# LayerNorm with GELU on one core: batch 3 loaded in one DMA, and 64 bytes written into the result by each DMA engine at the start

## The chip, the core and the metric

The kernel runs on one core of one Trainium2 chip. The metric is the device time of one execution in microseconds (us), less is better. Each number of a kernel is a median over several executions; repeated runs of one kernel here lie within 0.3% of each other, but for one run of 321.24 us.

## The reference

```python
# x: 8 x 1024 x 2048 float32; gamma, beta: 2048
mean = np.mean(x, axis=-1, keepdims=True)
var = np.var(x, axis=-1, keepdims=True)
normalized = (x - mean) / np.sqrt(var + eps)
out = gamma * normalized + beta
return 0.5 * out * (1 + np.tanh(np.sqrt(2 / np.pi) * (out + 0.044715 * out ** 3)))
```

67 MB go in and 67 MB come out.

## The kernel before

The 8192 rows are cut into 16 batches of 128 partitions times R = 4 rows. A batch is 4.19 MB and lives in one of five buffers, is normalized in place tile by tile (one tile is 128 rows, 1.05 MB), and is stored from the same buffer. SyncE issues all loads, ScalarE (ACT) all stores, so there are two data queues. Batch `b` uses buffer `(b + 4) % 5`; from batch 5 on a load waits until the store of the batch five before it has landed.

```python
# SyncE: loads
for b in range(B):
    s = slot(b)
    if stored(b):
        sy.wait_ge(s_store[s], stored(b))
    for q in range(R):
        if b == 0:
            sy.dma_start(out=xts[s][:, q:q + 1], in_=xg[0, :, q:q + 1]).then_inc(s_first[q], 16)
        elif b == SPLIT:      # SPLIT = 3: four DMAs in pieces of 8 KB
            sy.dma_start(out=xts[s][:, q:q + 1], in_=xg[b, :, q:q + 1]).then_inc(s_load[s], 16)
    if b not in (0, SPLIT):   # one DMA in pieces of 32 KB
        sy.dma_start(out=xts[s], in_=xg[b]).then_inc(s_load[s], 16 * R)
...
# ScalarE: scale and shift, GELU one tile later, then the store
for t in range(T + 1):
    ...
    ins = ac.activation(out=xt[:, q], in_=pss[i % 2], func=ACT.Gelu_apprx_tanh)._wait_ge(s_t, i + 1)
    if by_row(b):             # last batch: a store per tile, pieces of 8 KB
        ...
    elif q == R - 1:          # other batches: one store, pieces of 32 KB
        ins.then_inc(s_r, 1)
        ac.dma_start(out=og[b], in_=xt)._wait_ge(s_r, b + 1).then_inc(s_store[slot(b)], 16)
```

VectorE makes the statistics and multiplies by gamma, GpSimd makes the scale and the shift, TensorE adds beta in PSUM.

## Time and profile before

| | before |
|---|---|
| time, median of 3 runs | 319.97 us (319.55 to 320.1) |
| span of the profiled run | 318.3 us |
| bytes read and written | 134.26 MB, 422 GB/s over the span |
| busiest compute engine | ACT, 79% |
| DMA engines | 0.9 or more busy in 38 of 40 slices |

In the slices, a digit is the busy share of 1/40 of the span in tenths. In the windows used below, the columns are the stretch, its length, the busy time of PE, PE's weight loads, DVE, ACT and POOL with the number of instructions, the granted clock, the DMA share, and GB/s. A transfer piece counts as bytes where it starts, so with pieces of 32 KB on 16 engines a window of 2 us is coarse: one round of pieces is 0.52 MB.

Much of what follows rests on the trace's records of single transfers (start, duration, queue, size), which no view prints one by one. The prediction says how they are strung into 16 chains, one for each DMA engine; the program's known order of sizes is a check on it. What a chain's pieces take over their usual durations (309 ns for 8 KB, 1213 ns for 32 KB), and its gaps, I call its **loss**.

### The profile page before, as it was taken

To read this page: it belongs to the slowest core of one execution; us is meant where nothing else is said; L and a number is where in the kernel's file an instruction comes from. 1 tells how busy PE (TensorE), PEld (TensorE's weight loads), DVE (VectorE), ACT (ScalarE), POOL (GpSimd) and SP (SyncE) were. 2 spreads that over 40 slices of the span, in tenths; PEclk is the share of its full clock that TensorE was granted. 3 is DMA by queue.
4 is the path that set the end of the run, shared out by engine and by line. 5 is a ranking of instruction groups with operands and counts; after the bars stand their busy time and mean duration, and the time that the engine had idled before them with its cause. 6 is when DMAs were issued, how large, how long until landed. Compare 5 with 4: busy or idle time off the path is not lost.

```text
span 318.3 us, 2090 instructions
## 1 busy us (share of the span) xinstructions
PE 244.3 (77%) x520; PEld 57.1 (18%) x520; DVE 247.3 (78%) x386; ACT 251.7 (79%) x132; POOL 110.4 (35%) x201
## 2 busy tenths in 40 slices
PE   2769999999999989687796868959689596877850
PEld 1212222222212112111121112212112111211110
DVE  3499999999999898786968968699686987869710
ACT  2769999999999989698696977969599595986860
POOL 1144444444444444232442333343342442324300
DMA  7999999999999999999999999999999999999994
GB/s 287 441 453 406 389 433 436 441 416 449 420 436 445 413 449 416 445 428 432 449 408 453 416 449 424 432 449 412 453 416 445 428 428 445 420 445 424 436 401 204
DMA packets 6002, 134.26 MB, mean 422 GB/s; under 512 B 704, under 2 KB 752, under 8 KB 752
## 3 DMA queue, kind: packets, MB, share of 16 engines
q1 hardware_dynamic: 3168, 67.11, 49.5%
q10 hardware_dynamic: 2832, 67.13, 49.0%
q14 instruction: 2, 0.02, 0.0%
HBM read 67.13 MB, written 67.11 MB: 422 GB/s over the span
## 4 chain that ended last, share of the span: by engine, by line
DMA 64%; ACT 14%; DVE 10%; POOL 5%; PE 3%; issue 1%; ACTq 0%; DVEq 0%; POOLq 0%; SPq 0%
DMA out_dram<-xt 31%; DMA xt<-in_x_dram 31%; ACT yk L195 9%; DVE sts L149 7%; ACT xt L202 4%; POOL ves L135 3%; DVE zg L158 2%; PE ps L220 2%; DMA rows<-in_gamma_dram 2%; POOL rss L137 2%; POOL nms L139 1%; DVE mvs L155 1%; PE ps L237 1%; ACT g_t L191 1%; ACTq L205 0%
## 5 line engine op out<-in xcount | busy, mean ns | idle before, releaser
L149 DVE BATCH_NORM_STATS2 sts<-xt 128x6 f32<-128x512 f32 x256 | 157.7, 679 | 33.0 <-DMA xt<-in_x_dram 31.2
L195 ACT ACTIVATE yk<-xt,nms,rss 128x2048 bf16<-128x2048 f32 x64 | 133.8, 2090 | 47.9 <-POOL nms L139 41.9
L237 PE MATMUL ps<-zg,ident 128*128 128x512 bf16 x256 | 120.8, 627 | 54.8 <-DVE zg L158 53.8
L233 PE MATMUL ps<-b_hl,ones_b 33*128 33x512 bf16 x256 | 120.6, 624 | 2.2 <-PEq L228 2.2
L202 ACT ACTIVATE xt<-ps 128x2048 f32<-128x2048 f32 x64 | 119.0, 1859 | 1.5 <-PE ps L237 1.5
L135 POOL TENSOR_SCALAR ves<-mvs 128x1 f32<-128x1 f32 x64 | 38.4, 600 | 178.4 <-DVE mvs L155 178.4
L158 DVE TENSOR_TENSOR zg<-yk,g_t 128x2048 bf16<-128x2048 bf16 x64 | 76.4, 1194 | 19.2 <-ACT yk L195 19.2
L237 PEld LDWEIGHTS ps<-zg,ident 128*128 128x128 bf16 x256 | 27.6, 130 | 148.0 <-DVE zg L158 112.7
L233 PEld LDWEIGHTS ps<-b_hl,ones_b 33*128 33x128 bf16 x256 | 27.0, 127 | 92.1 <-issue 88.4
L139 POOL TENSOR_SCALAR nms<-mvs,rss 128x1 f32<-128x1 f32 x64 | 35.7, 558 | 6.3
L137 POOL TENSOR_TENSOR rss<-ves,mhalf 128x1 f32<-128x1 f32 x64 | 35.3, 552 | 5.3
L155 DVE BATCH_NORM_AGGREGATE mvs<-sts 128x2 f32<-128x24 f32 x64 | 16.9, 264 | 2.2
L220 PE MATMUL ps<-rows,ones 1*128 1x512 f32 x8 | 7.2, 1076 | 6.1 <-DMA rows<-in_gamma_dram 6.1
L188 ACT ACTIVATE b_hl<-rows 1x2048 bf16<-1x2048 f32 x1 | 1.9, 1910 | 5.2 <-DMA rows<-in_beta_dram 5.2
L166 DVE TENSOR_TENSOR b_hl<-rows,b_hl 1x2048 bf16<-1x2048 f32 x1 | 2.3, 2282 | 2.5 <-ACT b_hl L189 2.5
L220 PEld LDWEIGHTS ps<-rows,ones 1*128 1x128 f32 x8 | 2.5, 326 | 9.2 <-DMA rows<-in_gamma_dram 6.1
L191 ACT ACTIVATE g_t<-ps 128x2048 bf16<-128x2048 f32 x1 | 1.9, 1878 | 2.1 <-PE ps L220 2.1
L184 ACT ACT_TABLE_LOAD x1 | 1.3, 1283 | 0.9 <-SPq L107 0.9
L189 ACT ACTIVATE b_hl<-rows 1x2048 bf16<-1x2048 f32 x1 | 1.9, 1908 | 0.0
L161 DVE MEMSET b_hl<- 33x1024 uint32 x1 | 0.9, 912 | 1.2 <-SPq L107 1.2
L126 POOL MEMSET ones<- 65x128 f32 x1 | 0.2, 202 | 0.5 <-SPq L107 0.5
L130 POOL TENSOR_SCALAR_AFFINE_SELECT ident<-ident 128x128 bf16<-128x128 bf16 x1 | 0.3, 295 | 0.1
(7 smaller groups left out, 0.9 us busy)
## 6 DMA issues: line engine op xcount, KB each, us to landing
out_dram<-xt ACTq DMA_DIRECT2D x15, 4096.0 KB, 33.3
xt<-in_x_dram SPq DMA_DIRECT2D x14, 4096.0 KB
xt<-in_x_dram SPq DMA_DIRECT2D x8, 1024.0 KB, 8.2
out_dram<-xt ACTq DMA_DIRECT2D x4, 1024.0 KB, 9.0
rows<-in_beta_dram ACTq DMA_DIRECT2D x2, 8.0 KB, 5.8
rows<-in_gamma_dram ACTq DMA_DIRECT2D x1, 8.0 KB, 5.1
```

What stands on the lines that cost most here:

```text
L135: po.tensor_scalar(out=ves[:, c], in0=mvs[:, k, 1:2], scalar1=float(eps), scalar2=1.0, op0=ALU.add, op1=ALU.mult)._wait_ge(s_a, k + 1).the ...
L137: po.tensor_tensor(out=rss[:, c], in0=ves[:, c], in1=mhalf, op=ALU.pow)._wait_ge(s_q, 2 * k + 1).then_inc(s_q, 1)
L139: po.tensor_scalar(out=nms[:, c], in0=mvs[:, k, 0:1], scalar1=rss[:, c], scalar2=-1.0, op0=ALU.mult, op1=ALU.mult)._wait_ge(s_q, 2 * k + 2 ...
L149: ins = ve.bn_stats(out=sts[:, q, j, :], in_=xr[:, j, :])
L155: ve.bn_aggr(out=mvs[:, q], in_=sts[:, q])._wait_ge(s_o, count).then_inc(s_a, 1)
L158: ve.tensor_tensor(out=zgs[q % 2], in0=yks[q % 2], in1=g_t, op=ALU.mult)._wait_ge(s_n, count).then_inc(s_z, 1)
L191: ac.activation(out=g_t, in_=pss[0], func=ACT.Identity)._wait_ge(s_tg, 1).then_inc(s_c, 1)
L195: ac.activation(out=yks[t % 2], in_=xts[slot(b)][:, q], func=ACT.Identity, scale=rss[:, q:q + 1], bias=nms[:, q:q + 1])._wait_ge(s_p, t + ...
L202: ins = ac.activation(out=xt[:, q], in_=pss[i % 2], func=ACT.Gelu_apprx_tanh)._wait_ge(s_t, i + 1)
L220: ins = pe.matmul(pss[0][:, cols(j)], lhsT=ones[64:65], rhs=rows[64:65, j * K // nsub:(j + 1) * K // nsub, :d // K], start=True, stop=True)
L233: ins = pe.matmul(ps[:, cols(j)], lhsT=ones_b, rhs=b_hl[:, cols(j)], start=True, stop=False)
L237: ins = pe.matmul(ps[:, cols(j)], lhsT=ident, rhs=zgs[k % 2][:, cols(j)], start=False, stop=True)
```

## The change

The early write is meant to take an engine's first write to HBM, if such a write is slow, to the first microseconds. With that gone, batch 3 would no longer need to be loaded in small pieces beside the first store.

```diff
-SPLIT = 3
+    seed = sb("seed", [K, K], f32)                      # K = 16
+    s_seed = sem("seed")
...
-                        elif b == SPLIT:
-                            sy.dma_start(out=xts[s][:, q:q + 1], in_=xg[b, :, q:q + 1]).then_inc(s_load[s], 16)
-                    if b not in (0, SPLIT):
-                        sy.dma_start(out=xts[s], in_=xg[b]).then_inc(s_load[s], 16 * R)
+                    if b:
+                        sy.dma_start(out=xts[s], in_=xg[b]).then_inc(s_load[s], 16)
...
+                po.memset(seed, 0.0).then_inc(s_seed, 1)
...
+                ac.dma_start(out=og[0, 0:P:P // K, 0, 0:K], in_=seed)._wait_ge(s_seed, 1).then_inc(s_seed, 16)
                 ac.preload_act_table(ACT.Gelu_apprx_tanh)
...
+                    if i == R - 1:
+                        ac.wait_ge(s_seed, 17)
```

(VectorE's waits on `s_load` change from 64 to 16 with it.) The 16 early pieces go to rows of batch 0, which the first store overwrites; ScalarE waits for them before that store.

More of the change, by code (lines that the diff above doesn't have):

```diff
@@ L152, in stats @@
                             if wait[0] is s_load[s]:
-                                ins.then_inc(s_load[s], -16 * R)
+                                ins.then_inc(s_load[s], -16)
                     ins.then_inc(s_o, 1)
@@ L175, in _ @@
                         s, q = divmod(k, R)
-                        stats(s, q, (s_load[s], 16 * R) if q == 0 else None, k + 1)
+                        stats(s, q, (s_load[s], 16) if q == 0 else None, k + 1)
                         scale((q - 1) % R, k + 1)
```

## The prediction

> **What bounds the kernel now.** I read the page's slices first, because 134 MB pass through a kernel whose engines are all below 80% busy.
>
> ```profile
> PE 244.3 (77%) x520; PEld 57.1 (18%) x520; DVE 247.3 (78%) x386; ACT 251.7 (79%) x132; POOL 110.4 (35%) x201
> ...
> DMA  7999999999999999999999999999999999999994
> GB/s 287 441 453 406 389 433 436 441 416 449 420 436 445 413 449 416 445 428 432 449 408 453 416 449 424 432 449 412 453 416 445 428 428 445 420 445 424 436 401 204
> DMA packets 6002, 134.26 MB, mean 422 GB/s; under 512 B 704, under 2 KB 752, under 8 KB 752
> ```
>
> The DMA engines are full in every slice but the first and the last. So the time is bytes over rate, plus the start, plus the drain, plus whatever the 16 engines lose between. Second, the chain that ended last: nearly two thirds of it are transfers, half out and half in.
>
> ```profile
> DMA 64%; ACT 14%; DVE 10%; POOL 5%; PE 3%; issue 1%; ACTq 0%; DVEq 0%; POOLq 0%; SPq 0%
> DMA out_dram<-xt 31%; DMA xt<-in_x_dram 31%; ACT yk L195 9%; DVE sts L149 7%; ACT xt L202 4%; POOL ves L135 3%; DVE zg L158 2%; PE ps L220 2%; DMA rows<-in_gamma_dram 2%; POOL rss L137 2%; POOL nms L139 1%; DVE mvs L155 1%; PE ps L237 1%; ACT g_t L191 1%; ACTq L205 0%
> ```
>
> Third, the same chain in order of time. It ends in a string of ACT work, and that could mislead.
>
> ```profile
> 251.99 32.05 DMA xt<-in_x_dram
> ...
> 284.13 2.48 DVE sts L149 x4
> ...
> 307.45 1.88 ACT xt L202
> ```
>
> The last load lands at 284.0 and the last tile is computed by 309.3, when its 1 MB is issued; alone, 1 MB takes 2.4 us at 432 GB/s, but the span ends 9.0 us later. The store queue is backed up, so some 4 us of the compute tail are slack and the DMA engines set the end.
>
> Fourth, where they lose. The stretches of 2 us around the first store (issued at 36.05) are:
>
> ```profile
> 34.00:36.00 2.00, 1.94 (x6) 0.44 (x5) 1.97 (x4) 2.00 (x2) 1.38 (x2) 1.00 1.02 426
> 36.00:38.00 2.00, 2.00 (x6) 0.56 (x5) 1.97 (x5) 1.41 (x2) 0.48 (x2) 1.00 1.00 418
> 38.00:40.00 2.00, 1.29 (x4) 0.15 (x1) 1.46 (x3) 2.00 (x2) 1.53 (x3) 1.00 1.13 348
> 40.00:42.00 2.00, 1.98 (x5) 0.56 (x6) 2.00 (x4) 2.00 (x2) 0.10 (x1) 1.00 0.97 397
> ```
>
> The last column falls from 426 to 348 GB/s while the DMA share stays full: engines are occupied but slow. The trace's 6000 single transfer records on the two data queues show why. On one engine the next record starts 3 to 4 ns before the last ends, so they can be strung into 16 chains. An 8 KB piece of a load takes 309 ns; between 38.0 and 40.5, just ahead of each engine's first store piece, pieces take up to 754 ns. Summed over each chain from 35 to 42 us (time over the usual duration, and the gaps), an engine loses 0.24 to 1.35 us there, **0.83 us in the mean**. No other store does that: from 42 to 62, where the second store starts, the mean is 0.13. The first reads, before 5 us, show the like: 0.02 to 1.04 us, mean 0.53.
>
> Last, the drain: 14 of the 16 chains end between 313.7 and 314.6 us, one at 315.3, one at 316.6. The span ends 1.7 us after that one. It lost 1.26 us at the first store, and 2.35 us more in small excesses from 100 us on.
>
> **What the Trainium skill says.** DMA: Bandwidth & Descriptors, "Queues, rings and completion order": each engine takes turns between the queues it has work for, packet by packet. The trace agrees: after 40 us a chain alternates one 8 KB load piece with one 32 KB store piece, so the first store gets four fifths of the bandwidth. That is what the split of buffer 3 buys. The same page, "Why a DMA increments its semaphore by 16 and not by 1": the slowest dimension sets how many engines serve a DMA, 16 at most. The new write has 16 rows, so one piece of 64 bytes and one increment for each engine; the parameter rows, also cut in 16, show the pattern, 3 pieces and 3 increments on each engine. Its "Specifications" say that below 512 B a transfer is a read-modify-write; no run yet shows what a 64-byte write costs. HBM Reference, "Specifications (TRN2)", gives some 425 GB/s for a core that streams alone; here it is 422 over the span. I found no page that says that a first write is slower than later ones.
>
> **The change part by part.**
>
> The whole load of batch 3. Per engine, 32 pieces of 8 KB (309 ns, less 3.3 of overlap, so 9.78 us) and 4 increments (9 ns each, some 6 net) become 8 pieces of 32 KB (1213 ns, 9.68 us) and 1 increment: 9.80 becomes 9.68, **0.12 us less**, all on the bound. SP issues one DMA in place of four, beside other work. The first store loses its privilege: piece for piece it now gets half of 432 GB/s. From 40 us its 4.19 MB take 19.5 us and not the 14.5 that the trace shows; it lands near 60, not at 55. Load 5, which waits for that, is issued 5 us later. Does its queue run dry? At 40 us some 1 MB of batch 3 is still to come, then batch 4: 5.2 MB at 216 GB/s last to 64. It doesn't, by some 4 us, and if it did, store 1 (issued at 52.4) would have the engines to itself. So this only exchanges bytes between the directions: loads are some 6 us earlier from then on, stores later. **0 us**.
>
> The early write. On Pool a memset of 16 x 16, 0.1 us like the memset of one column, beside the start. On ACT one DMA issue, 0.61 us by gamma's row, ahead of gamma and beta, and a wait for the memset of some 0.2 us. Gamma lands at 6.04 now and starts the PE work up to 13.3, g_t at 15.2 and all that follows, so compute moves by 0.6 to 1 us until the chain meets the transfers at 68.8. Loads to fill the engines are queued until 64, so nothing runs dry: **0 us on the end**. The pieces cost each engine some 27 + 9 ns, as a parameter row does: **+0.03 us**. The wait for its landing before the first store costs nothing: it has had 30 us.
>
> What the write is for. If the loss at the first store belongs to an engine's first write to HBM, it goes from 38 us: **-0.7 us** (0.83, less the 0.13 that a store start still shows at the second store). But it doesn't vanish: the engines already have loads at 2 us, so a stall at the start is also DMA time, unless it lies beside the stall of the first reads (1.9 to 3.4 us). The write is issued some 0.2 us behind the first load, so it should overlap in part. I choose a third surviving: **+0.25 us**.
>
> Sum: -0.12 + 0.03 - 0.70 + 0.25 = -0.54, so **319.4 us**.
>
> **The rivals.**
>
> (a) The stall only moves. It costs at 4 us what it cost at 39. For it: gamma's first piece ran at 5.0 us, behind nine records of the load, so the write too may come after the first reads have recovered. Against it: 64 bytes, not 32 KB, are in flight. Then -0.12 + 0.03: 319.9.
>
> (b) The loss at the first store is not of a first write but of turning from loads alone to both directions, or of the read of SBUF. For it: the second store, which met loads after the first had ended on some engines, shows 0.13. Against it: it is six times smaller. Then the early write is wasted, and with loads in 32 KB pieces the start of the first store may cost more: 319.9 to 320.4.
>
> (c) The late chain decides. The end is that of one engine, 2 us behind the middle of the others, and it lost 1.26 us at the first store. If the lateness is in the order in which the engines were put out of step there, a start without the stall draws them anew: as good as 318.0, or no gain.
>
> (d) The first store's share mattered after all: a slot free 5 us later starves compute. Against it: compute takes 16.4 us per batch (stores issued at 36.05 and 52.44), the transfers 19.5, and loads come sooner, not later. I give it one chance in fifty of a visible loss.
>
> **Range and chances.** The middle is the sum. (a) and (b) put the upper edge at 320.2, a little over the highest run of before, 320.1. Everything going well, the stall gone and hidden and the late chain 0.5 us nearer, gives 318.4. Two per cent are 6.4 us; nothing that is taken away has that size (all losses over the usual durations are some 3 us per engine), and to lose it a new idle stretch would be needed: 0.01 faster, 0.98 same, 0.01 slower.
>
> **What would show it.** In the profile after: the slices stay full; windows from 38 to 42 hold near 430 GB/s; the store's pieces alternate with 32 KB load pieces; the first store takes some 23 us to land in place of 18.9; the last load lands some 6 us before 284; gamma lands at 6.6 to 7; the early window from 2 to 6 us loses a few hundred ns per engine. I'm wrong if the dip at the first store stays (then b), if the early windows lose as much as the dip did (a), if a DMA slice falls below 9 in the middle (d), or if the chains' mean end moves as said but the last chain doesn't (c).

## The result

| | runs | median | range |
|---|---|---|---|
| before | 6 | 319.98 us | 319.55 to 320.34 |
| changed | 6 | 319.67 us | 319.54 to 320.3 |

The ratio of the changed kernel to the one before is 0.9995, with a 95% interval of 0.9982 to 1.0008: the same.

The page of the changed kernel, its slices and its chain of what ended last:

```profile
DMA  7999999999999999999999999999999999999995
GB/s 285 445 450 413 450 389 421 446 421 441 425 433 450 418 446 417 441 425 433 441 421 450 421 441 425 437 433 425 450 421 446 417 446 425 433 437 425 446 397 222
DMA packets 5602, 134.26 MB, mean 423 GB/s; under 512 B 688, under 2 KB 736, under 8 KB 736
...
DMA 45%; ACT 19%; DVE 18%; POOL 9%; PE 3%; issue 2%; ACTq 1%; POOLq 0%; DVEq 0%; SPq 0%
```

The engines are as full as before. The transfers' share of the chain has fallen from 64% to 45%, with hardly a change of the time: the chain follows inferred releases back from the last instruction, and compute work that runs beside full queues can carry it. It doesn't say what the kernel is bound by when a resource is full all along.

The chain of the changed kernel in order of time (start, duration, what) at the start and at the end:

```profile
0.93 0.11 POOL seed L125
1.06 0.39 ACTq L185
1.51 5.49 DMA rows<-in_gamma_dram
7.01 0.04 issue
7.05 7.20 PE ps L224 x8
...
135.45 41.63 DMA out_dram<-xt
177.09 25.57 DMA xt<-in_x_dram
...
254.52 26.18 DMA xt<-in_x_dram
...
304.10 1.88 ACT xt L206
```

Gamma lands 1 us later, at 7.0, and compute starts that much later. A load takes 26 us from issue to landing and not 32 to 34, a store 42 and not 36: bytes have changed places between the directions. The last load lands at 280.7 in place of 284.0 and the last tile is done at 306.0 in place of 309.3, yet the span ends at 317.7, 0.6 us sooner. Compute was not what set the end.

The windows of the changed kernel around its first store, which is issued at 37.0:

```profile
34.00:36.00 2.00, 2.00 (x6) 0.42 (x4) 1.97 (x4) 2.00 (x2) 0.51 (x1) 1.00 1.14 492
36.00:38.00 2.00, 1.95 (x6) 0.43 (x4) 2.00 (x4) 1.41 (x2) 1.34 (x3) 1.00 0.87 377
38.00:40.00 2.00, 2.00 (x5) 0.42 (x4) 1.43 (x4) 2.00 (x2) 0.68 (x2) 1.00 1.27 442
40.00:42.00 2.00, 1.27 (x4) 0.43 (x4) 2.00 (x3) 2.00 (x2) 0.94 (x2) 1.00 0.74 262
42.00:44.00 2.00, 2.00 (x6) 0.42 (x4) 1.97 (x5) 2.00 (x2) 0.32 (x1) 1.00 1.12 475
```

The dip is still there, at 40 to 42. These windows are coarse now, so I go by the chains. The last load piece or two of each engine ahead of its first store piece take up to 1950 ns in place of 1213. The mean loss per engine, from the transfer records, in ns, by stretches in us from the span's start (two last columns: mean and last end of the 16 chains, us):

```
kernel        0-5   5-12  12-35  35-44  44-62  62-100  100-320   mean end  last end
before        531     51     94    836    133      63      191     314.3     316.6
changed       589     53     56    820     60      24      160     314.1     315.9
```

The loss at the first store is unchanged: 836 and 820.

### The profile page after: what moved, and what is told of

It reads as the page before. It is cut to its first block, busy times and chain, and to the rows that moved or that the text cites. A ratio compares the mean times of both kernels' runs of the same rounds, so it can differ in the third digit from the quotient of the medians.

```text
span 317.7 us, 2090 instructions
## 1 busy us (share of the span) xinstructions
PE 244.3 (77%) x520; PEld 57.2 (18%) x520; DVE 247.1 (78%) x386; ACT 251.4 (79%) x132; POOL 110.5 (35%) x202
## 4 chain that ended last, share of the span: by engine, by line
DMA 45%; ACT 19%; DVE 18%; POOL 9%; PE 3%; issue 2%; ACTq 1%; POOLq 0%; DVEq 0%; SPq 0%
DMA out_dram<-xt 27%; DMA xt<-in_x_dram 16%; ACT yk L197 14%; DVE sts L149 11%; ACT xt L206 5%; DVE zg L158 5%; POOL ves L135 5%; POOL rss L137 3%; PE ps L224 2%; DMA rows<-in_gamma_dram 2%; POOL nms L139 1%; DVE mvs L155 1%; PE ps L241 1%; ACT g_t L193 1%; ACTq L209 0%
```

## The experiments

### The two parts alone, and both together

`seed_only` is the kernel before plus the early write; `whole_only` is the changed kernel without it:

```diff
-                po.memset(seed, 0.0).then_inc(s_seed, 1)
-                ac.dma_start(out=og[0, 0:P:P // K, 0, 0:K], in_=seed)._wait_ge(s_seed, 1).then_inc(s_seed, 16)
-                    if i == R - 1:
-                        ac.wait_ge(s_seed, 17)
```

> Undoes the whole load of batch 3 and keeps the early 64-byte write. Theory T1 (the loss of 0.8 us per engine at the first store is not one of a first write, so the early write does nothing for it): chains lose 0.7 to 0.9 us each between 35 and 44 us as in the kernel before, ratio to before 0.999 to 1.001. Theory T2 (the early write does help, and the whole load hides it by making the start of the first store dearer): the loss between 35 and 44 us falls below 0.4 us and the time falls by 0.4 us or more (ratio 0.9985 or less).

> Undoes the early write and keeps the whole load. T1: same loss at the first store as in the kernel after, 0.8 us; time equal to the kernel after within noise, 319.7 (ratio 0.9985 to 1.0). T2: the loss at the first store is larger than after, 1.2 us or more, and the time above before's.

Both were then checked again: the changed kernel as it is in `after_again`, and in `after_third` in the same rounds as the whole load alone (`whole_again`).

> The changed kernel once more, for more runs and for a second trace. T1 (the early write is idle): ratio to before like whole_only's 0.9984, within 0.001. If the early write costs something: above 0.9990, as in its first runs (0.9995).

> The whole load alone once more, on the same chip and in the same rounds as the changed kernel. If the early write is idle but for its own cost of under 0.1 us: ratio to before 0.998 to 0.9995, equal to after_third's within 0.0005. If the early write costs the third of a stall that I predicted (0.25 us): whole_again faster than after_third by 0.0008 or more.

> The changed kernel beside whole_again. Equal to it within 0.0005 if the early write is idle; slower by 0.0008 or more (0.25 us) if the write costs DMA time at the start.

| kernel | median us | before, same rounds | ratio, 95% interval |
|---|---|---|---|
| seed_only | 320.28 | 320.2 | 1.0005 (0.9991 to 1.0018) |
| whole_only | 319.69 | 320.2 | 0.9984 (0.9971 to 0.9998) |
| changed (after_again) | 319.94 | 319.91 | 1.0003 (0.9989 to 1.0017) |
| whole_again | 319.74 | 320.13 | 0.9992 (0.9978 to 1.0005) |
| changed (after_third) | 319.76 | 320.13 | 0.9990 (0.9976 to 1.0003) |

```
kernel        0-5   5-12  12-35  35-44  44-62  62-100  100-320   mean end  last end
seed_only     546     52     92    866    107      23      233     314.4     316.7
whole_only    525     80     83    725     61      26      166     313.9     316.2
whole_again   524     90     84    649     59      29      194     313.9     316.2
after_again   435     58     62    632     59      35      163     313.8     315.9
after_third   524     55     69    865     57      26      166     314.0     316.3
```

The early write does nothing: 866 with it and 836 without it beside the split, 632 to 865 with it and 649 to 725 without it beside the whole load. Nor do the traces show a cost within the span: beside the whole load the last chains end at 315.9 to 316.3 with it and at 316.2 without it. In the shared rounds the two kernels are 0.0002 apart, under the 0.0005 that I had set, but each interval is some 0.0013 wide to either side. My T2, that it helps and something hides it, fell with `seed_only`.

There is a cost outside the span, though. The record gives the time and, to 0.1 us, the span of each timed run. In all timed runs of the experiments without the early write (before, whole_only, whole_again, low_engines, rebalance) the time is 1.73 to 1.86 us longer than the span, 1.8 in the mean. With it the mean is 2.0 us in the changed kernel's first runs, in `seed_only` and in `after_again`, and 1.9 in `after_third`. So the early write costs some 0.1 to 0.2 us before the first or after the last instruction that the profile counts; where is not shown. (The single runs of `probe` and `probe2`, with early stores of another kind, have 1.9 and 2.0.) That is why `after_again` came out at 1.0003, above the 0.9990 that I had set as a sign of a cost: its spans are 0.2 us shorter than before's in the mean, and this takes them back.

The whole load shifts the mean end of the chains from 314.3 or 314.4 (before, seed_only) to 313.8 to 314.1 (the five traces with it), about 0.4 us. The whole load without the early write gives ratios of 0.9984 and 0.9992, in the mean 0.4 us less too. One interval of five excludes 1, just; the rest do not. The gain stands in all five traces and is at the edge of what the times can show.

### Is it a place that the engine has not touched?

`seed128` writes 64 bytes of every row and from every partition that the first store will use, and not only 16:

```diff
-    seed = sb("seed", [K, K], f32)
+    seed = sb("seed", [P, K], f32)
-                ac.dma_start(out=og[0, 0:P:P // K, 0, 0:K], in_=seed)
+                ac.dma_start(out=og[0, :, 0, 0:K], in_=seed)
```

> The early write made of 128 rows of 64 bytes instead of 16, so every engine reads each SBUF partition and writes each 32 KB row that its first store piece will use. If the loss at the first store is that of addresses or partitions that the engine had not touched: under 0.3 us per engine between 35 and 44 us. If not: 0.7 to 0.9 as in the kernel after.

The chains lose 724 ns each between 35 and 44 us. So it isn't a matter of rows or partitions touched for the first time, as far as 64 bytes of each row of 32 KB can show it.

### Is it the second queue's start?

`load_on_act` has the load of batch 4 issued on ACT's queue, so that this queue starts with 4 MB of load:

```diff
-                    if b:
+                    if b and b != 4:
...
+                ac.dma_start(out=xts[slot(4)], in_=xg[4]).then_inc(s_load[slot(4)], 16)
                 for t in range(T + 1):
```

> whole_only, with the load of batch 4 issued from ScalarE's queue at about 15 us, so that the second queue starts with a load. If the loss is one of the second queue's first large pieces, whatever the direction: 0.5 us or more per engine between 16 and 22 us. If it belongs to stores: under 0.2 us there, and 0.6 us or more at the first store, around 38 to 43 us.

From 16 to 22 us, where the queue starts, the loss is 22 ns; from 40 to 46, at the first store, it is 575 ns. So a first start of the queue with a load is free, and the price comes with stores. (The 575 ns are a little under the 0.6 I had set, and this is one trace.)

The same trace holds a second stall, which I had overlooked. The third store is issued at 72.17 us. No store piece starts between 75.8 and 77.7, and the load pieces there take up to 2584 ns:

```profile
74.00:76.00 2.00, 1.41 (x4) 0.22 (x2) 1.43 (x4) 2.00 (x2) 1.41 (x3) 1.00 0.80 344
76.00:78.00 2.00, 1.86 (x5) 0.48 (x6) 2.00 (x5) 2.00 (x2) 0.21 (x1) 1.00 1.29 410
78.00:80.00 2.00, 1.95 (x6) 0.49 (x6) 1.97 (x4) 2.00 (x2) 1.07 (x2) 1.00 0.77 328
```

From 76 to 80 us an engine loses 703 ns in the mean, more than the 575 at the first store. By then the queue had carried 4 MB of load and nearly all of two stores, so being first is not needed for the stall.

### Is it paid once, or at every start of stores?

`probe` puts a store of 1 MB of raw x ahead, to rows of the last batch, which are overwritten later; loads run alone again for some 20 us before the first real store:

```diff
+                for q in range(R):
+                    ac.wait_ge(s_first[q], 16)
+                ac.dma_start(out=og[B - 1, 0:32], in_=xts[slot(0)][0:32]).then_inc(s_probe, 16)
                 ac.activation(out=g_t, in_=pss[0], ...)
...
+                    if i == 0:
+                        ac.wait_ge(s_probe, 16)
```

> whole_only plus an early store of 1 MB of raw x (32 rows of 32 KB, so two pieces of 32 KB per engine) at about 13 us, overwritten later; loads alone run again from about 19 us until the first real store at about 37. T1a (the loss is that of turning from loads alone to loads and stores, every time): about 0.8 us per engine at 14 to 19 us AND again 0.5 to 0.8 at 38 to 43. T1b (the loss belongs to the first large store of all): 0.8 us at 14 to 19 us, under 0.2 at 38 to 43. The kernel takes 2.4 us or so longer for its extra 1 MB either way.

`probe2` has two such stores, alike, of the tile `xts[slot(0)][:, 3:4]` in pieces of 8 KB:

> whole_only with two equal early stores of 1 MB (8 pieces of 8 KB per engine) at about 13 and about 26 us, loads alone between them, then the real first store at about 39. If what remains after the first big store (0.28 us in probe) is the price of every start of stores after a pause: 0.2 to 0.4 us at the second and at the real one alike. If the loss wears off with each start: second larger than third, third under 0.15.

```
mean loss per engine, ns          first start     second start    third start
probe   (32 KB pieces)            569 (15-22 us)  276 (38-46)
probe2  (8 KB, 8 KB, then 32 KB)  348 (16-24)       6 (31-38)     222 (48-56)
```

Neither of my pairs of theories holds as I put it. In `probe` the second start is dearer than "once" and cheaper than "every time". In `probe2` the loss doesn't wear off in order, and the starts aren't alike either. What can be said: the first store costs 350 to 870 ns by run and piece size. A later start costs anything from 6 ns to the 703 of the third store in `load_on_act`; between them lie 222 and 276 here and 317 at the real second store of `probe2` (82 to 86 us). A store queued behind others mostly costs nothing that I can see, but in `tags`, below, 136 and 188 ns are lost where one store ends and the next begins (76 to 82 and 193 to 198 us). What makes one start dear and another free is not settled. None of this can gain anything here: an early store large enough to take the first price costs more than it saves. (The DMA engines have no time to spare: `probe` took 322.17 us.)

### Which engine ends last?

In every trace of the two kernels one chain ends some 2 us behind the median of the 16 (before: 316.6 and 314.1; changed: 315.9 and 313.9). `tags` adds 14 tiny loads behind the last load, on 2 to 15 rows, so that a chain shows its engine's number by how many it carries:

```diff
+                for k in range(2, K):
+                    sy.dma_start(out=tags[0:k, k, :], in_=xg[0, 0:k, 0, 0:K]).then_inc(s_tag, 16)
```

> The changed kernel with 14 tiny loads of k rows (k from 2 to 15) of 64 bytes behind the last load, so that a chain of transfers carries 15 - e tags where e is its engine's number (14 for engines 0 and 1). It tells which engine ends last, 2 us behind the others. If it is a property of an engine: the same as in the next runs, and its store pieces take 1226 ns and more in place of 1213 to the end. Time within 0.5 us of the kernel after.

The counts came out as 14 twice and 13 down to 0 once each. The last chain carries 11 of them. By the rule of the Trainium skill (DMA: Bandwidth & Descriptors, "Why a DMA increments its semaphore by 16 and not by 1"), by which a DMA of k rows, up to 16, from SP or ACT runs on the k lowest-numbered engines, that is engine 4; the trace prints no engine numbers, so the number rests on the page, while the nested counts agree with it. It is one trace on one chip; the slow chains of the other runs have no number. From 275 us on, all 25 of that chain's 32 KB pieces take more than the usual 1213 ns (1216 to 1268); on all other chains, none. In the traces of the changed kernel, too, a slow chain takes 1226 to 1260 ns for most store pieces, from the first 50 us to the end.

### Two tries to spare that engine

`low_engines` gives 32 rows of one of the last four stores to DMAs of 4 rows, `rebalance` issues 120 rows of another from GpSimd. Both start from whole_only:

```diff
# low_engines, third tile from the end
+                            ac.dma_start(out=og[b, 0:96, q:q + 1], in_=xt[0:96, q:q + 1])...
+                            for p in range(96, P, 4):
+                                ac.dma_start(out=og[b, p:p + 4, q:q + 1], in_=xt[p:p + 4, q:q + 1]).then_inc(s_low, 16)
# rebalance, second tile from the end
+                po.dma_start(out=dummy, in_=xg[0, 0:5, 0, 0:K]).then_inc(s_sw, 16)
+                po.dma_start(out=og[B - 1, 0:120, 2:3], in_=xts[slot(B - 1)][0:120, 2:3])...
```

> whole_only with 32 of the 128 rows of one of the last four stores given to eight DMAs of 4 rows each, which should run on engines 0 to 3 only: those get 6 more pieces of 8 KB (1.8 us), the other twelve 2 fewer (0.6 us). Engine 4, which ends 2 us after the others (tags), ends 0.6 us sooner, engines 0 to 3 about level with it. If the end is that of engine 4: 0.6 us less than whole_only, ratio to before about 0.997. If the end follows the mean of the engines: no gain, ratio 0.9984 or so.

> whole_only with 120 of the 128 rows of the third of the last four stores issued from GpSimd behind a tiny 5-row load, in the hope that they then run on 15 engines without engine 4 (the other 8 rows on engines 0 to 7). If they do: engine 4 has 7 pieces of 8 KB less (2.1 us), the last chain ends level with the rest near 314.5 and the ratio to before is about 0.993. If the 15 engines are 0 to 14: engine 15 is spared, engine 4 is not, and the time is whole_only's (0.9984). Should the DMA from GpSimd start slowly it is hidden behind the queue of stores.

`low_engines`: 322.21 us against 319.91, ratio 1.0078 (1.0064 to 1.0091): slower, clear of noise. Two lines of its list of DMA issues (count, KB each, us from issue to landing) show the split store; the eight small ones are parts of the tile of which the first carries three quarters:

```profile
out_dram<-xt ACTq DMA_DIRECT2D x1, 768.0 KB, 13.6
out_dram<-xt ACTq DMA_DIRECT2D x8, 32.0 KB
```

Four chains carry the eight small stores, and the slow chain is not among them, which agrees with engine 4. But from 306 to 313 us 8 KB store pieces on some chains take up to 874 ns in place of 309. One of the four chains loses 2.2 us in that way, another 1.3, and the slow one 1.4. So the end moves out, to 318.5. Why the small stores, or what follows them, do this is open.

`rebalance`: 320.35 us against 319.91, ratio 1.0014 (1.0000 to 1.0027). The chain without GpSimd's pieces ends at 311.8 us, spared as meant, but it is another one: the slow chain has its 8 pieces and ends at 316.6. This agrees with the same section of the skill, by which a DMA from GpSimd can give each engine a sixteenth of the rows, rounded up: 8 pieces on each of 15 chains, none on one. Here too, 8 KB pieces lose time while two queues store at once, up to 982 ns for one, 0.39 us per engine in the mean from 304 us on. So neither try beat the whole load alone.

## Why the prediction was right or wrong

The time is within the range (319.67 against 319.4 and 318.4 to 320.2), and the class is right. The way there is half wrong, and that the number fits is in part luck: two errors covered each other.

**The bound** was right. The DMA engines are full throughout, compute could start 1 us later and finish 3.3 us sooner, and neither moved the end by that much.

**"The whole load of batch 3": the mechanism right, the term too small.** The 0.12 us that I worked out from piece durations are part of it. The chains' mean end moves by 0.4, because the losses fall as well: from 44 to 62 us from 133 or 107 ns to 60, and at the first store perhaps by 0.1 us (836 and 866 with the split; 632 to 865 in the five traces with the whole load, and 681 to 724 in `seed128`, `tags`, `low_engines` and `rebalance`, which have it too; they overlap). The rest is scattered over the run, in stretches with differences of 10 to 70 ns that single traces can't settle. Why the losses fall is not shown.

**"The first store loses its privilege" and nothing runs dry**: right. By the trace's semaphore increments batch 3 has landed at 45.5 us and batch 4 at 64.9 (I had 64 for batch 4), and the engines stay full. The first store lands 25.2 us after its issue, not 23, and the last load 3.3 us sooner, not 6: compute holds the pace longer, as the chain's first transfer after the start comes at 135.4 us and not at 68.8.

**"Compute moves by 0.6 to 1 us"**: right, 0.95 us by gamma's landing and by the first store's issue, and free.

**"If the loss at the first store belongs to an engine's first write": wrong.** This is the step that failed, as -0.70, and with it the +0.25 that I let survive. Neither 16 nor 128 early rows changed the loss, and the early write brought none at the start: 546 ns from 0 to 5 us in seed_only, 531 in the kernel before. Their sum was -0.45 us; it is 0.0 within the span, and the write's 0.1 to 0.2 us outside the span, which no term foresaw, come near the +0.25 by luck. What ran in its place is rival (b) in part: the loss comes at starts of stores among loads, though not at each, and not at the first alone, as `load_on_act` shows. But (b)'s fear that it would cost more with loads of 32 KB did not come true. Why such a start stalls stays open.

**Rival (c)**, the late chain, is right in what it says of the end and wrong in its cause. The end follows one engine, 2 us behind. It is behind because its store pieces are 1 to 4% longer all along, and not by what it lost at the first store.

So -0.54 was made of -0.12 (which is -0.4 in the mean end of the chains) and -0.42 (which is 0 within the span and +0.1 to +0.2 outside it). The three ratios of the changed kernel, 0.9995, 1.0003 and 0.9990, average to 0.9996, or 0.1 us less; -0.4 and +0.2 come to that within the scatter of the times.

Three slips in the prediction moved nothing: all losses are 1.9 us per engine by the table's first row, not some 3; rival (b) reached to 320.4, beyond the range's edge of 320.2; and its "buffer 3" is batch 3, which lies in buffer 2.

## What to carry to other kernels

A dip in the bandwidth at a first event looks like a price of being first; before building a warm-up, start the same thing twice with a pause between, start the queue in the other direction, and look through the whole of each trace for the same stall: in `load_on_act` it came back at 76 us, outside the window that was asked for. With full DMA engines, keep a ledger by engine: it turns a difference of 0.1% that the times barely show into terms that can be read one by one, and it shows which engine ends last. Compare the time with the span as well: a cost outside the span is in no trace. Large pieces were worth some 0.1% here, for one batch in sixteen, as the queues did not run dry by it.

## What the Trainium skill lacked or had wrong

- **DMA: Bandwidth & Descriptors**, "Latency and other measured facts", says that engines 7 and 15 are usually the slower ones, guesses at descriptors written by GpSimd as the cause, and calls this specific to such DMAs. It names no slow engine for these. In both kernels here all DMAs come from SP and ACT, and one engine is slow all the same, in `tags` number 4 by the page's rule of counting: mostly 1226 to 1260 ns for a 32 KB store piece where others take 1213, so that it ends 2 us behind the others' 314.
- The same page says nothing of what a start of stores among running loads costs: 0.58 to 0.87 us per engine for a first store of 4 MB here, 0.35 to 0.57 for a first store of 1 MB, 0.01 to 0.70 for later starts. A start of the second queue with a load cost 0.02.
- Its "Specifications" call writes under 512 B read-modify-writes; 16 rows of 64 bytes each took 11 ns in the records, landed after 3.8 us by the profile page's list of issues, and left no loss that can be told from scatter.
- No page that I read says that 8 KB store pieces can lose time while several small stores, or the stores of two queues, are in flight: up to 874 ns for a piece in `low_engines` and 982 in `rebalance`, in place of 309. The cause is not shown.
